# First layer's opening: normalised tiles emitted whole, and the order of projections and modulation vectors

## The chip, the cores and the metric

The kernel runs on one core of one Trainium2 chip. The metric is the device time of the whole kernel in microseconds (us); the median of three runs stands for it. TensorE (PE in the profile) does the matmuls, VectorE (DVE), ScalarE (ACT) and GpSimd (POOL) do the elementwise work, and SyncE (SP) issues most DMA transfers.

## The reference, cut to what matters

Two layers of a diffusion backbone over 512 latent tokens and 256 context tokens, 1024 features wide. Only the opening of the first layer bears on this change: a vector product that gives shift and scale for each feature, a normalisation of the tokens, and the first columns of the input projection.

```python
mod_x = silu_c @ ada_w[layer] + ada_b[layer]          # the latent tokens' vectors
mod_c = silu_cc @ ada_w[layer] + ada_b[layer]         # the context tokens' vectors
sh1, sc1, g1, sh2, sc2, g2 = [m[:, None, :] for m in jnp.split(mod_x, 6, axis=-1)]
csh1, csc1, cg1, csh2, csc2, cg2 = jnp.split(mod_c, 6, axis=-1)
hx = modulate(rmsnorm(x, norm1_g[layer]), sh1, sc1)   # h * (1 + scale) + shift
hc = modulate(rmsnorm(ctx, norm1_g[layer]), csh1, csc1)
lat, cx = project_in(hx, w_in[layer]), project_in(hc, w_in[layer])   # hx @ w_in
```

All that follows (retention, gated linear attention, output projection, the MLP, the second layer) starts from these projections.

## The kernel before, in words

Tokens lie along the free axis (768 columns: latent 0 to 511, context 512 to 767) and features along the 128 partitions, so the stream is 8 feature blocks, numbered kk. Every large matmul is done as products of a high and a low part: a weight slab is split into `hi_wi` (ScalarE, L244) and `lo_wi` (VectorE, L245), and a normalised tile into `hh_n` (ScalarE) and `hl_n` (VectorE). `project` (L443 to L447 and L459, L460) issues three matmuls for each feature block (hi x hi, hi x lo, lo x hi); for slab 0 (`RankSlab`) it issues two, L459 on `hh_n` and L460 on `hl_n`.

The first layer opens by quarters, because its modulation vectors come from 8 MB of `ada_w` that must be loaded first. A quarter q covers feature blocks 2q and 2q + 1 and has these steps:

- the vector product (`quarter`, L391): 32 matmuls of the conditioning vectors with the quarter's share of `ada_w` (eight loads of 256 KB), summed in the one bank of the pool `psa`;
- `ada_finish`: ScalarE copies the row out (`adarow`, L269), TensorE transposes it (`adat`, L274), VectorE adds the bias into `mod` (L280). It is a generator: it starts with the copy, the second tick after that emits the transposes, the third emits the additions;
- `quarter_end`: VectorE forms the scales (`mods_n`, L507);
- `quarter_norm`: queues four tile chains, latent kk = 2q and 2q + 1, then context 2q and 2q + 1. A chain (`apply`) has three steps, one a tick: x times rstd (VectorE L525, or GpSimd L518 where kk is 2 or 5), then `hh_n` on ScalarE (L527, or L520 and L521), then `hl_n` on VectorE (L529 or L523). One chain is started each tick, so four chains are wholly emitted after six ticks;
- the projections (`start_project`): slabs 0, 1 and 3, each on the latent and then on the context columns, accumulate over all four quarters in six PSUM banks (`acc0`). Below, "slab 1's block" is both groups of one slab for one quarter.

Each engine works through its own instructions in the order in which the program emits them. `project` calls `ready` on each tile first, which ticks the chains until that tile's chain is emitted, and it ends with one tick. So before this change the order of emission was, for quarters 2 and 3: vector product, row copy, then the projections of the quarter before, with the transposes and the additions emitted inside them by the ticks. For quarter 2 the four tile chains of quarter 1 were still unemitted when its vector product was issued.

SyncE issues the loads in one queue: x of the latent tokens, quarter 0, slabs 0, 1 and 3, x of the context tokens, quarters 1, 2 and 3, and then the slabs of the first token projection (`ps_vg`, slabs 5 to 8), which follows the opening. Their splits are emitted after quarter 3's tiles.

Of the kernel before, what the change touches and what calls it, by code (L numbers as in the profile page):

```python
# [138 lines left out]
def build(ctx: ExitStack, tc, a):  # L139
# [15 lines left out]
    ch = Chains()  # L155

    def bank(name):
        return ps.tile([P, 512], F32, tag="ps", name=name)
# [21 lines left out]
    ALLG = [(0, LAT), (LAT, T)]  # L180
# [84 lines left out]
    def ada_finish(l, pt, tiles, n, fold=1):  # L265

        m = 32 * fold * len(tiles)
        row = temp(f"adarow_{l}_{tiles[0]}")
        nc.scalar.copy(row[0:m, 0:n], pt[0:m, 0:n])  # L269
        yield  # L270
        yield
        tt = bank(f"adat_{l}_{tiles[0]}")
        for j in range(n // P):
            nc.tensor.transpose(tt[:, j * P : j * P + m], row[0:m, j * P : (j + 1) * P], ident[0:m, 0:m])  # L274
        yield
        src = tt.rearrange("p (j c m) -> p j c m", j=4, c=4)
        for i in range(fold * len(tiles)):
            f = tiles[i % len(tiles)]
            dst = mod[l][:, :, f : f + n // P]
            nc.vector.tensor_tensor(  # L280
                dst, src[:, 0 : n // P, i, 0:2].rearrange("p j v -> p v j"),
                dst if i >= len(tiles) else rep(adab[:, l, f : f + n // P], 2), op=ALU.add,
            )
# [99 lines left out]
    def quarter(q, middle=None, end=None):  # L383

        pt = psa.tile([P, 512], F32, tag="psa", name=f"ada0_{q}")
        for k2 in range(KK // 2):
            if k2 == 2 and middle:
                middle()
            for c in range(4):
                kk = 2 * k2 + c // 2  # L390
                nc.tensor.matmul(  # L391
                    pt[32 * c : 32 * c + 32, 0:QF], cs[:, kk, :], quarter_w[q, kk][:, c % 2],
                    start=(k2 == 0), stop=(k2 == KK // 2 - 1),
                )
        if end:
            end()
        return ch.start(ada_finish(0, pt, [2 * q, KK + 2 * q], QF, 2))
# [51 lines left out]
    def project(pt, slab, c0, acts, t0, t1, ks=None, first=0, last=None):  # L449

        ks = range(len(acts)) if ks is None else ks
        last = len(acts) - 1 if last is None else last
        out = pt[:, 0 : t1 - t0]
        for k in ks:
            acts[k].ready(ch, t0, t1)
            xh, xl = acts[k].hi[:, t0:t1], acts[k].lo[:, t0:t1]
            w = slice(c0 + k * P, c0 + k * P + P)
            if isinstance(slab, RankSlab):
                nc.tensor.matmul(out, slab.hi[:, w], xh, start=k == first, stop=False)  # L459
                nc.tensor.matmul(out, slab.hi[:, w], xl, start=False, stop=k == last)  # L460
            else:
                mm3(out, slab.hi[:, w], slab.lo[:, w], xh, xl, k == first, k == last)
        ch.tick()
# [87 lines left out]
    def squares(t0, t1, late=KK):  # L551
        for kk in range(KK):
            if kk < late:
                norm0.add_square(kk, t0, t1, kk == 0)
            else:
                norm0.late_square(kk, t0, t1)
            if kk:
                ch.tick()

    def fill(n):  # L560

        pt = bank(f"fill{n}")
        for _ in range(n):
            nc.tensor.matmul(pt[:, 0:P], ones_d, ones_d, start=True, stop=True)

    def quarter_norm(q, groups):
        for t0, t1 in groups:
            norm0.apply_all(0, 0, int(t0 > 0), t0, t1, (2 * q, 2 * q + 1))

    def quarter_end(q, chain):  # L570
        ch.finish(chain)
        norm0.scales(0, 8, n1g, 2 * q, 2 * q + 2)

    START = (0, 1, 3)
    acc0, quarter_chain = {}, {}

    def start_project(q, groups):
        for j in START:
            for t0, t1 in groups:
                if q == 0:  # L580
                    acc0[j, t0] = bank(f"ps0_{j}_{t0}")
                project(acc0[j, t0], sl0[j], 0, norm0.out, t0, t1, (2 * q, 2 * q + 1), 0, KK - 1)

    def start_norms():
        squares(0, LAT)
        end = quarter(0, lambda: norm0.stat(0, LAT))
        sl0[0].cast()
        quarter_end(0, end)
        fill(12)
        quarter_norm(0, ALLG[:1])  # L590
        for _ in range(2):
            ch.tick()
        sl0[0].low()
        for _ in range(2):
            ch.tick()
        sl0[1].split()
        sl0[3].split()
        squares(LAT, T, 5)
        start_project(0, ALLG[:1])
        norm0.stat(LAT, T)  # L600
        quarter_norm(0, ALLG[1:])
        for _ in range(6):
            ch.tick()
        end = quarter(1)
        start_project(0, ALLG[1:])
        quarter_end(1, end)
        quarter_norm(1, ALLG)
        quarter_step(2)
        quarter_finish(2)

    def quarter_step(q):
        quarter_chain[q] = quarter(q)
        start_project(q - 1, ALLG)

    def quarter_finish(q):
        quarter_end(q, quarter_chain[q])
        quarter_norm(q, ALLG)
        for _ in range(6):
            ch.tick()

    late = {}
# [46 lines left out]
    def layer(l, norm):  # L668
# [436 lines left out]
        if l == 0:  # L1105

            def head():
# [5 lines left out]

            plan = [
                Item(pre + "norm", start_norms, ahead=0),
                Item(pre + "q3", lambda: quarter_step(3), ahead=0),
                Item(pre + "q3n", lambda: quarter_finish(3), ahead=0),
                Item(pre + "q3p", lambda: start_project(3, ALLG), ahead=0),
                Item(pre + "head", head, ahead=4),
# [340 lines left out]
```

## Time and profile before

| | |
|---|---|
| median of 3 runs | 1656.87 us (1656.79 to 1657.32) |
| profiled execution: its own time | 1658.22 us |
| span in the trace | 1656.5 us |
| PE busy | 1622.8 us, 98% of the span |
| DVE, ACT, POOL busy | 943.8, 628.7, 191.9 us |
| mean granted clock of TensorE | 0.996 |
| first vector product starts | 11.92 us |
| first matmul of `ps_vg` (the opening is over) | 64.17 us |

The table's times are microseconds from the start of the span. A granted clock of 1.00 is TensorE's upper level, 2.4 GHz, and 0.50 is the lower, 1.2 GHz. A busy share says how long an engine had an instruction in work, not that it worked at its peak.

### The profile page before, as it was taken

The page shows a single profiled execution, that of the slowest core. Times are in us where ns is not written, and L with a number is a line of the kernel's source. Part 1 is how long each engine was busy: PE and PEld are TensorE (multiplying, and loading weights), DVE is VectorE, ACT ScalarE, POOL GpSimd, SP SyncE. Part 2 cuts the span into 40 slices and gives each one's busy share as a digit, 9 for nine tenths or more (in the row PEclk, how much of TensorE's full clock was granted, in tenths as well). Part 3 has the DMA queues.
Part 4 walks back from the last instruction along what each step waited for, and adds up shares of the span by engine and source line. Part 5 has one row for each costly group of instructions (what it writes and reads, how often), then busy time and mean ns, then how long its engine had stood idle before and what let it go on. Part 6 is the DMA issues. An engine that isn't in the chain of part 4 may idle for free. (4 is left out here: it accounts for less than half of the span.)

```text
span 1656.5 us, 23002 instructions
## 1 busy us (share of the span) xinstructions
PE 1622.8 (98%) x9290; PEld 1386.3 (84%) x9290; DVE 943.8 (57%) x1494; ACT 628.7 (38%) x1085; POOL 191.9 (12%) x213
## 2 busy tenths in 40 slices
PE   6999999999999999999999999999999999999997
PEld 3778788988998888888888887888889988888887
DVE  4776564554756565555556476688466743443445
ACT  4545423662542221222222247363464622222232
POOL 2000021210111000110101121002111301010010
PEclk9999999999999999999999999999999999999999
DMA  9433333123323343333333221121114323223311
GB/s 318 155 127 127 129 109 115 57 67 112 103 88 124 103 136 100 125 115 115 128 114 118 96 99 64 51 65 64 51 57 147 115 89 102 94 97 102 102 64 52
DMA packets 57483, 173.82 MB, mean 105 GB/s; under 512 B 6208, under 2 KB 17792, under 8 KB 57376
## 3 DMA queue, kind: packets, MB, share of 16 engines
q1 hardware_dynamic: 54944, 164.32, 29.9%
q0 software_dynamic: 2432, 8.03, 1.4%
q8 instruction: 73, 1.20, 0.3%
q14 instruction: 34, 0.28, 0.1%
HBM read 168.13 MB, written 4.19 MB: 104 GB/s over the span
## 5 line engine op out<-in xcount | busy, mean ns | idle before, releaser
L446 PE MATMUL pm<-yl,hi_m 128*128 128x512 f32 (+1 forms) x808 | 279.8, 346 | 1.1 <-DVE yl L523 0.7
L445 PE MATMUL pm<-yh,hi_m 128*128 128x512 f32 (+1 forms) x808 | 279.9, 346 | 0.0
L445 PE MATMUL pm<-hidh,hi_m 128*128 128x512 f32 (+1 forms) x800 | 279.1, 349 | 0.0
L447 PE MATMUL pm<-yh,lo_m 128*128 128x512 f32 (+1 forms) x808 | 278.7, 345 | 0.0
L446 PE MATMUL pm<-hidl,hi_m 128*128 128x512 f32 (+1 forms) x800 | 278.4, 348 | 0.0
L447 PE MATMUL pm<-hidh,lo_m 128*128 128x512 f32 (+1 forms) x800 | 277.3, 347 | 0.0
L1231 ACT ACTIVATE relu<-pm 128x512 f32<-128x512 f32 (+1 forms) x101 | 51.2, 507 | 494.1 <-PE pm L447 490.4
L1235 DVE TENSOR_TENSOR hidl<-relu,hidh 128x512 fp32r<-128x512 f32 (+1 forms) x101 | 61.6, 612 | 289.9 <-POOL relu L1233 289.9
L543 DVE SCALAR_TENSOR_TENSOR x<-pm,mod,x 128x512 f32<-128x512 f32 (+1 forms) x200 | 117.6, 640 | 109.0 <-PE pm L447 109.0
L1233 POOL TENSOR_TENSOR relu<-relu 128x512 f32<-128x512 f32 (+1 forms) x101 | 90.5, 897 | 756.0 <-ACT hidh L1232 755.8
L446 PEld LDWEIGHTS pm<-yl,hi_m 128*128 128x128 f32 x808 | 153.1, 189 | 20.7 <-DVE yl L529 1.2
L445 PEld LDWEIGHTS pm<-yh,hi_m 128*128 128x128 f32 x808 | 153.1, 189 | 19.9 <-issue 1.2
L445 PEld LDWEIGHTS pm<-hidh,hi_m 128*128 128x128 f32 x800 | 151.5, 189 | 21.2 <-issue 1.1
L447 PEld LDWEIGHTS pm<-yh,lo_m 128*128 128x128 f32 x808 | 153.0, 189 | 18.7
L447 PEld LDWEIGHTS pm<-hidh,lo_m 128*128 128x128 f32 x800 | 151.1, 189 | 19.6
L446 PEld LDWEIGHTS pm<-hidl,hi_m 128*128 128x128 f32 x800 | 151.5, 189 | 18.9 <-issue 0.2
L245 DVE TENSOR_TENSOR lo_m<-raw_m,hi_m 128x1024 fp32r<-128x1024 f32 x126 | 153.9, 1222 | 10.1 <-ACT hi_m L244 10.1
L244 ACT CAST hi_m<-raw_m 128x1024 fp32r<-128x1024 f32 x128 | 129.5, 1041 | 51.3 <-DMA raw_m<-in_w_mlp 28.3
L351 DVE SCALAR_TENSOR_TENSOR adaacc<-adaw,cs,adaacc 128x1024 f32<-128x1024 f32 x84 | 103.9, 1278 | 0.0
L245 DVE TENSOR_TENSOR lo_wi<-raw_wi,hi_wi 128x1024 fp32r<-128x1024 f32 x54 | 66.4, 1246 | 27.7 <-ACT hi_wi L244 27.6
L445 PE MATMUL pwo<-yh,hi_wo 128*128 128x256 f32 (+1 forms) x224 | 70.9, 316 | 0.1
L446 PE MATMUL pwo<-yl,hi_wo 128*128 128x256 f32 (+1 forms) x224 | 70.3, 314 | 0.3 <-DVE yl L1079 0.3
(307 smaller groups left out, 2937.7 us busy)
## 6 DMA issues: line engine op xcount, KB each, us to landing
raw_m<-in_w_mlp SPq DMA_DIRECT2D x128, 512.0 KB, 3.5
adaw<-in_ada_w SPq DMA_DIRECT2D x80, 512.0 KB, 3.8
raw_wi<-in_w_in SPq DMA_DIRECT2D x58, 512.0 KB, 4.2
adaw<-in_ada_w SPq DMA_DIRECT2D x32, 256.0 KB, 6.1
raw_wo<-in_w_out SPq DMA_DIRECT2D x16, 512.0 KB, 3.5
x<-in_xT POOLq DMA_DIRECT2D x8, 384.0 KB, 8.1
x<-in_xT SPq DMA_DIRECT2D x8, 256.0 KB, 5.3
raw_wob<-in_w_out SPq DMA_DIRECT2D x4, 512.0 KB, 4.4
```

The costliest lines, as they stand in the source:

```text
L244: nc.scalar.copy(self.hi, self.raw)
L245: self.engine.tensor_sub(self.lo, self.raw, f32(self.hi))
L351: nc.vector.scalar_tensor_tensor(acc[:, v], w, c, acc[:, v], op0=ALU.mult, op1=ALU.add)
L445: nc.tensor.matmul(out, wh, xh, start=first, stop=False)
L446: nc.tensor.matmul(out, wh, xl, start=False, stop=False)
L447: nc.tensor.matmul(out, wl, xh, start=False, stop=last)
L543: nc.vector.scalar_tensor_tensor(xs[kk][:, t0:t1], pt[:, 0 : t1 - t0], mod[l][:, v, gate + kk : gate + kk + 1], xs[kk][:, t0:t1], op0=ALU. ...
L1231: nc.scalar.activation(r, pt[:, 0 : t1 - t0], AF.Relu)
L1233: nc.gpsimd.tensor_mul(r, r, r)
L1235: nc.vector.tensor_sub(a_.lo[:, t0:t1], r, f32(a_.hi[:, t0:t1]))
```

## The change

`start_project` takes a list of slabs. In `quarter_step` the projections of the quarter before are cut in two: those of slabs 0 and 1 are issued ahead of the next quarter's vector product, those of slab 3 behind it. After quarter 1's tile chains are queued, eight ticks emit them whole before quarter 2's step. `quarter_finish` ticks eight times in place of six.

```diff
-    def start_project(q, groups):
-        for j in START:
+    def start_project(q, groups, slabs=START):
+        for j in slabs:
...
         quarter_norm(1, ALLG)
+        for _ in range(8):
+            ch.tick()
         quarter_step(2)
         quarter_finish(2)
 
     def quarter_step(q):
+        start_project(q - 1, ALLG, START[:2])
         quarter_chain[q] = quarter(q)
-        start_project(q - 1, ALLG)
+        start_project(q - 1, ALLG, START[2:])
 
     def quarter_finish(q):
         quarter_end(q, quarter_chain[q])
         quarter_norm(q, ALLG)
-        for _ in range(6):
+        for _ in range(8):
             ch.tick()
```

## Rows read from the trace of the kernel before

**Rows 1.** The page's busy times and shares of the span.

```profile
PE 1622.8 (98%) x9290; PEld 1386.3 (84%) x9290; DVE 943.8 (57%) x1494; ACT 628.7 (38%) x1085; POOL 191.9 (12%) x213
```

**Rows 2.** PE by stages: stage, length, busy (instructions), clock, DMA share, GB/s.

```profile
0.00:50.00 50.00, 33.70 (x198) 0.93 0.92 308
50.00:100.00 50.00, 49.73 (x265) 1.00 0.31 105
```

**Rows 3.** PE's waits after 64 us, longest: total, times, longest us.

```profile
PE ps_d L459 <- ACT hh_n L527: 1.5, 1, 1.5
```

**Rows 4.** PE's timeline of the opening: start, us, instruction [idle before, releaser].

```profile
34.43 4.43 PE L391 MATMUL ada<-adaw,cs 128*32 128x256 f32 x32
39.33 0.44 PE L274 MATMUL adat<-c_ident,adarow 128*128 128x128 f32 x2 [0.47 <-ACT adarow L269]
40.04 0.50 PE L459 MATMUL ps<-hh_n,hi_wi 128*128 128x512 f32 x1 [0.27 <-ACT hh_n L520]
41.78 0.79 PE L460 MATMUL ps<-hl_n,hi_wi 128*128 128x512 f32 x1 [1.24 <-DVE hl_n L523]
...
44.52 0.63 PE L445 MATMUL ps<-hh_n,hi_wi 128*128 128x512 f32 x1
...
50.43 1.93 PE L391 MATMUL ada<-adaw,cs 128*32 128x256 f32 x32
52.30 0.50 PE L459 MATMUL ps<-hh_n,hi_wi 128*128 128x512 f32 x1
...
53.80 0.38 PE L274 MATMUL adat<-c_ident,adarow 128*128 128x128 f32 x2
53.94 0.47 PE L445 MATMUL ps<-hh_n,hi_wi 128*128 128x512 f32 x1
...
59.97 0.39 PE L445 MATMUL ps<-hh_n,hi_wi 128*128 128x512 f32 x1
...
64.17 0.40 PE L445 MATMUL ps_vg<-hi_wi,hh_n 128*128 128x512 f32 x1
```

**Rows 5.** Weight loads' timeline, the last wait of quarter 2's product.

```profile
38.23 0.14 PEld L391 LDWEIGHTS ada<-adaw,cs 128*32 128x32 f32 x4 [0.62 <-DMA adaw<-in_ada_w]
```

**Rows 6.** VectorE's timeline of the opening.

```profile
34.28 0.23 DVE L507 SCALAR_TENSOR_TENSOR mods_n<-mod,c_n1g 128x2 f32<-128x2 f32 x2
...
43.58 0.47 DVE L529 SCALAR_TENSOR_TENSOR hl_n<-xn_n,mod,hh_n 128x256 fp32r<-128x256 f32 x1
43.98 0.22 DVE L507 SCALAR_TENSOR_TENSOR mods_n<-mod,c_n1g 128x2 f32<-128x2 f32 x2
...
48.78 0.42 DVE L523 TENSOR_TENSOR hl_n<-xn_n,hh_n 128x256 fp32r<-128x256 f32 x1 [0.44 <-ACT xn_n L521]
...
54.69 0.23 DVE L507 SCALAR_TENSOR_TENSOR mods_n<-mod,c_n1g 128x2 f32<-128x2 f32 x2
...
59.21 0.48 DVE L529 SCALAR_TENSOR_TENSOR hl_n<-xn_n,mod,hh_n 128x256 fp32r<-128x256 f32 x1 [0.18 <-ACT hh_n L527]
60.14 4.63 DVE L245 TENSOR_TENSOR lo_wi<-raw_wi,hi_wi 128x1024 fp32r<-128x1024 f32 x4 [0.45 <-ACT hi_wi L244]
```

**Rows 7.** ScalarE's timeline: quarter 1's first tile.

```profile
39.17 0.82 ACT L520 ACTIVATE hh_n<-xn_n,mod,mods_n 128x512 fp32r<-128x512 f32 x1
```

**Rows 8.** PE in half-microsecond stages where the granted clock changes; columns of rows 2.

```profile
41.00:41.50 0.50, 0.00 (x0) 0.78 1.13 367
48.00:48.50 0.50, 0.50 (x5) 0.90 0.06 25
1003.50:1004.00 0.50, 0.29 (x2) 0.84 0.27 90
1007.00:1007.50 0.50, 0.50 (x6) 0.75 0.00 0
```

**Rows 9.** PE's timeline at the second layer's opening.

```profile
995.40 0.70 PE L498 MATMUL st_n<-ssum_n,ones_d 128*128 128x256 f32 x2 [1.29 <-DVE ssum_n L481]
...
1001.29 0.38 PE L459 MATMUL ps_d<-hh_n,hi_wi 128*128 128x256 f32 x1 [1.53 <-ACT hh_n L527]
```

## The prediction

> **What bounds the kernel now.** I read the page first, then TensorE's share by stages of 50 us, then the waits, and only then the opening's timelines. TensorE is busy 98% of the span [rows 1], so time is lost or won only where it waits or runs at its lower clock. The stages say where that is: the first 50 us hold 16.3 us in which TensorE had no matmul, at a mean clock of 0.93, and the next 50 us hold 0.3 [rows 2]. Of all its waits after 64 us the longest is 1.5 us, for a tile at the second layer's opening [rows 3], and no DMA is among the releasers. Hence a shift of the point where the opening ends and `ps_vg` begins, 64.17 us [rows 4], goes through to the end of the kernel nearly one for one: no later wait for a load is there to swallow it.
>
> In the opening itself the reader sees this [rows 4]. Quarter 2's vector product takes from 34.43 to 38.86, 4.43 us for work that takes 1.93 at quarter 3, because it runs at the pace of its loads; the last of them is waited for until 38.23 [rows 5]. ScalarE's row copy of quarter 2 stands behind that product and ahead of quarter 1's tiles, so quarter 1's first `hh_n` starts only at 39.17 [rows 7]. TensorE then waits again, 1.24 us for `hl_n` [rows 4], and its clock falls: the half microsecond from 41.0 has a mean of 0.78, and the one from 48.0 a mean of 0.90 on its way up [rows 8], so it was at 0.50 from about 41.3 to 48.05. From 50.43 on TensorE has nearly no gap until 64.17: quarter 3's product, quarter 2's six projections with quarter 3's transposes inside them, quarter 3's projections.
>
> So two things are to be weighed: the stretch of 10.1 us from 34.43 to 44.52, in which TensorE does a product and slab 0's block only, and the cover that the later quarters have now.
>
> **Step 1: quarter 1's tiles come earlier.** With the tiles emitted before the vector product, the row copy no longer stands ahead of them. They need the scales, which end at 34.28 + 0.23 = 34.51 [rows 6]. Before, the four tiles took from 39.17 [rows 7] to 43.58 + 0.47 = 44.05 [rows 6], 4.88 us, with ScalarE and VectorE in turn. From 34.55 that gives 39.43. Slab 1's block starts 0.28 us behind the last tile (59.21 + 0.48 = 59.69 to 59.97 [rows 6, 4]), so at 39.7 where it was 44.52: 4.8 us won. GpSimd's products need no scales and stay off this path.
>
> **Step 2: two blocks, the product, one block.** At the upper clock the blocks of slabs 1 and 3 take 64.17 - 59.97 = 4.20 us together [rows 4], 2.10 each. A product with its weights present takes 52.30 - 50.43 = 1.87 [rows 4], and quarter 2's are present from about 38.3 [rows 5]. So 39.7 + 2.10 + 1.87 + 2.10 puts quarter 2's transposes at 45.8. The wait for the loads is covered.
>
> **Step 3: what is late next.** `ada_finish` emits its transposes on its second tick and its additions on the third. Behind the product there are now two projections, hence two ticks, so the transposes come behind all of the quarter's projections and nothing is left on TensorE to cover what follows them: additions, scales, four tiles. All of quarter 2's projections stand behind that in TensorE's queue, and so do quarter 3's product and everything later. The price comes from before, where the same chain ran under cover. From transposes to scales: 54.69 - 53.80 = 0.89 [rows 6, 4]. From quarter 2's scales to its last tile: 48.78 + 0.42 - 43.98 = 5.22 [rows 6]. With the 0.28 of step 1 that is 6.4 us until slab 1's block, in which TensorE has only its transposes and slab 0's block to do (53.80 - 52.30 = 1.50 [rows 4]): about 4.7 us of new idle time. Block, product and block (6.07) put quarter 3's transposes at 45.8 + 6.4 + 6.1 = 58.3. Quarter 3's chain from transposes to slab 1's block took 59.97 - 53.80 = 6.17 [rows 4], which gives 64.4, and two blocks of 2.10 end the opening at 68.6. At the upper clock throughout, the change costs 68.6 - 64.17 = 4.4 us: it wins 4.8 once and some of the first clock loss, and then pays two gaps of 4.5 to 4.7 that were under cover.
>
> **Step 4: the clock.** Two falls in this trace give the price. In the opening the blocks of slabs 1 and 3 took 50.43 - 44.52 = 5.91 in place of 4.20 [rows 4], a loss of 1.7. At the second layer the clock fell at about 1003.8 and rose at about 1007.25 [rows 8], 3.4 us of dense matmuls at half speed, again 1.7. It fell there after a wait of 1.53 us at 1001.29 with lone matmuls behind it, while a single wait of 1.29 at 995.40 did not bring it down [rows 9]. The new order has three stretches of 5 to 6 us (after the projections of quarters 0, 1 and 2, each up to the last tile of the next quarter) in which TensorE is idle for 3.8, 4.7 and 4.5 us: each idles longer than either stretch before which the clock fell. I count three falls. Bounds for each: nothing, if it does not fall, and 3.4, if dense work meets all of a low stretch as long as the opening's 6.8 us. I take 2.0, near the two rows, a little above as the blocks behind each gap are longer than those at the second layer. Three times 2.0 is 6.0; what before lost to its own fall is already in the 64.17.
>
> The Trainium skill, "TensorE: Matmul & The Clock Gate", section "HAM oscillation — how this bites in real kernels", speaks against this change: bursts with waits between them make every burst start at the lower clock, and the cost is paid at each. By that rule the sum is the whole 4.4 + 6.0; by the 995.40 row alone, where a wait passed without a fall, it is 4.4.
>
> **Edits at nothing.** The two extra ticks in `quarter_finish` find the four chains done. No DMA is added or moved on SyncE's queue or GpSimd's. The splits of slabs 5 to 8 follow quarter 3's last tile (60.14 for 4.63 us [rows 6]) and move with it; `ps_vg` keeps its distance to them, since two blocks still lie between. If that cover failed, each split would show as up to 1.2 us of wait (4.63 / 4).
>
> **The sum.** 4.4 + 6.0 = 10.4 us. On the profiled execution, 1658.22 (span 1656.5), that is 1668.6; its own time lies 1.35 above the median, so on the median of 1656.87 the forecast is 1667.3.
>
> **The rivals.** (a) The gaps come, but TensorE's clock stays up, or falls once: 4.4 to 6.4 us, 1661.3 to 1663.3. For it: lone matmuls break each gap, the first stretch is the only one like the one that fell before, and a wait of 1.29 us passed [rows 9]. Against it: the idle sums above. (b) The falls are long ones, each near 3.4: 14.6 us, 1671.5. For it: the opening's own low stretch was that long [rows 8]. Against: half of such a stretch falls into waiting. (c) Faster: the transposes' chain is covered after all, so that only step 1 works. Then the opening ends at 45.8 + slab 0's block, block, product, block (7.6) + slab 0's block and two blocks (5.7) = 59.1, about 5 us earlier, 1651.8. It turns on the two gaps: below 2.4 us each the change would win. Against it: after its transposes TensorE has no instruction that does not need a tile of that quarter, and the first `hh_n` alone needs additions, scales, one product and one ScalarE pass. (d) No change to speak of: the gaps come out at half their price with no fall, or a later wait swallows the shift; 1657 to 1660. Against it: [rows 2, 3].
>
> **How the numbers follow.** The forecast 0.61, (a) 0.18, (b) 0.12, (c) 0.04, (d) 0.05. A measurement here tells about 0.2%, 3.3 us, from no change; so slower has 0.61 + 0.18 + 0.12 = 0.91, the same 0.05, faster 0.04. The forecast's own range is 1664.5 to 1670. The range given runs from below (a), with the gaps some tenths cheaper, to (b): 1660.5 to 1671.5.
>
> **What would show it.** Step 1: quarter 1's first `hh_n` near 34.6, slab 1's block near 39.7 to 40. Step 2: quarter 2's product with no wait for DMA, in 1.9 us (up to double at the lower clock). Step 3: two stretches, each starting at L274, with some 2.2 us of no matmul until `hh_n` and the rest of the idle time behind `hl_n`. Step 4: three stretches of granted clock 0.50 before 75 us. `ps_vg` starts near 74.6. The prediction is wrong if transposes stand ahead of a block, if `ps_vg` starts by 66, or if the shift at `ps_vg` is not that at the end.

## The result, and the profile after

The changed kernel takes 1667.14 us (median of 4 runs, 1666.03 to 1668.68) against 1656.83 for the kernel before: 10.3 us slower, a ratio of 1.0063 with a 95% interval of 1.0046 to 1.0081. The forecast was 1667.3. The profiled execution of the changed kernel took 1666.81, that of before 1658.22, so the two traced executions differ by 8.6 us and not by 10.3; the section on the prediction comes back to this.

TensorE's timeline of the opening, changed kernel (start, us, instruction, idle before and its releaser):

```profile
35.35 0.49 PE L459 MATMUL ps<-hh_n,hi_wi 128*128 128x512 f32 x1 [0.92 <-ACT hh_n L520]
36.93 0.50 PE L460 MATMUL ps<-hl_n,hi_wi 128*128 128x512 f32 x1 [1.08 <-DVE hl_n L523]
...
39.35 0.39 PE L460 MATMUL ps<-hl_n,hi_wi 128*128 128x256 f32 x1 [1.13 <-DVE hl_n L523]
...
40.82 0.63 PE L445 MATMUL ps<-hh_n,hi_wi 128*128 128x512 f32 x1
...
44.07 1.93 PE L391 MATMUL ada<-adaw,cs 128*32 128x256 f32 x32
...
48.17 0.38 PE L274 MATMUL adat<-c_ident,adarow 128*128 128x128 f32 x2
50.80 0.50 PE L459 MATMUL ps<-hh_n,hi_wi 128*128 128x512 f32 x1 [2.26 <-ACT hh_n L527]
...
54.72 0.63 PE L445 MATMUL ps<-hh_n,hi_wi 128*128 128x512 f32 x1
...
57.87 1.93 PE L391 MATMUL ada<-adaw,cs 128*32 128x256 f32 x32
...
61.94 0.38 PE L274 MATMUL adat<-c_ident,adarow 128*128 128x128 f32 x2
64.58 0.49 PE L459 MATMUL ps<-hh_n,hi_wi 128*128 128x512 f32 x1 [2.26 <-ACT hh_n L527]
...
68.26 0.63 PE L445 MATMUL ps<-hh_n,hi_wi 128*128 128x512 f32 x1
...
71.38 0.40 PE L445 MATMUL ps<-hh_n,hi_wi 128*128 128x512 f32 x1
...
73.48 0.40 PE L445 MATMUL ps_vg<-hi_wi,hh_n 128*128 128x512 f32 x1
```

These rows answer to [rows 4]. Quarter 2's vector product at 44.07 takes 1.93 us with no wait for a load, where it took 4.43. Quarter 1's first tile meets TensorE at 35.35, where it was 40.04. Then come two stretches that were not there before: behind the transposes at 48.17 and at 61.94 TensorE has no matmul for 2.26 us, waits again inside slab 0's block, and reaches slab 1's block 6.55 and 6.32 us after the transposes. `ps_vg` starts at 73.48, 9.3 us later.

TensorE by stages of the changed kernel (stage, length, busy, granted clock, DMA share, GB/s):

```profile
40.00:50.00 10.00, 8.12 (x60) 0.84 0.67 253
50.00:60.00 10.00, 8.10 (x53) 0.83 0.10 28
60.00:70.00 10.00, 6.95 (x27) 0.85 0.00 1
```

The mean clock is 0.83 to 0.85 in each of three stages: it fell three times in this execution, each time for about 3.4 us, where the opening of the kernel before has one fall of 6.8 us [rows 8]. Slab 1's block, 2.10 us at the upper clock, takes 44.07 - 40.82 = 3.25, 57.87 - 54.72 = 3.15 and 71.38 - 68.26 = 3.12.

### The profile page after: what moved, and what is told of

The parts are those of the page before. It is cut to its first block, busy times and chain, and to the rows that moved or that the text cites. A ratio compares the mean times of both kernels' runs of the same rounds, so it can differ in the third digit from the quotient of the medians.

```text
span 1665.0 us, 23000 instructions
## 1 busy us (share of the span) xinstructions
PE 1624.1 (98%) x9290; PEld 1387.4 (83%) x9290; DVE 945.3 (57%) x1494; ACT 629.1 (38%) x1085; POOL 192.0 (12%) x213
```

## The experiments

Each kernel was timed together with the kernel before, whose medians were 1655.8 to 1656.7; the ratios are to these. Each edit is shown against the changed kernel, that of e6 against e1. All keep the eight ticks of `quarter_finish`, so no run tests these by themselves.

**e1: the early tiles without the new order.**

```diff
     def quarter_step(q):
-        start_project(q - 1, ALLG, START[:2])
         quarter_chain[q] = quarter(q)
-        start_project(q - 1, ALLG, START[2:])
+        start_project(q - 1, ALLG)
```

> Only the eight ticks that emit quarter 1's tiles whole; the vector product stands ahead of all six projections again. Theory (the new order uncovers the chain behind the transposes, the early tiles win time): slab 1's block of quarter 1 near 40.8 us in place of 44.52, no gap behind the transposes of quarters 2 and 3, ps_vg near 59 to 61, kernel at 1652 to 1654. Rival A (the early tiles themselves cost: TensorE idles before slab 1's block and its clock falls there): 1657 to 1660, not below the kernel before.

Measured: 1652.7 us (1652.2 to 1653.45), ratio to before 0.9976 (0.9967 to 0.9986). TensorE's timeline of e1, and its stage with the clock:

```profile
34.09 3.46 PE L391 MATMUL ada<-adaw,cs 128*32 128x256 f32 x32
...
40.40 0.38 PE L274 MATMUL adat<-c_ident,adarow 128*128 128x128 f32 x2
40.54 0.48 PE L445 MATMUL ps<-hh_n,hi_wi 128*128 128x512 f32 x1
...
44.92 1.93 PE L391 MATMUL ada<-adaw,cs 128*32 128x256 f32 x32
...
48.32 0.38 PE L274 MATMUL adat<-c_ident,adarow 128*128 128x128 f32 x2
...
58.68 0.40 PE L445 MATMUL ps_vg<-hi_wi,hh_n 128*128 128x512 f32 x1
```

```profile
40.00:50.00 10.00, 9.82 (x76) 1.00 0.77 279
```

The product is paced by its loads again (3.46 us), but it now runs while quarter 1's tiles are made, so slab 1's block starts at 40.54 in place of 44.52 [rows 4]. The transposes stand ahead of that block, two blocks (four projections) of cover follow, there is no gap behind them, and the clock stays at 1.00 in the opening. The early tiles win 4.0 us; rival A, that they cost, is out.

**e2: the new order without the eight ticks.**

```diff
         quarter_norm(1, ALLG)
-        for _ in range(8):
-            ch.tick()
         quarter_step(2)
```

> Only the new order of projections, without the eight ticks behind quarter 1's chains. Theory: the projections emit the tiles by their own ticks ahead of the product, so nothing moves: the same two gaps of 4.5 to 5 us behind the transposes, ps_vg near 73.5, 1666 to 1668. Rival A (the ticks carry the cost): near the kernel before, 1657 to 1659.

Measured: 1667.47 us (1666.55 to 1668.48), ratio 1.0066 (1.0051 to 1.0081). TensorE's timeline of e2:

```profile
47.91 0.38 PE L274 MATMUL adat<-c_ident,adarow 128*128 128x128 f32 x2
50.55 0.50 PE L459 MATMUL ps<-hh_n,hi_wi 128*128 128x512 f32 x1 [2.26 <-ACT hh_n L527]
...
73.25 0.40 PE L445 MATMUL ps_vg<-hi_wi,hh_n 128*128 128x512 f32 x1
```

The same gap of 2.26 us and nearly the same end of the opening (73.25 against 73.48). The order carries the whole loss; with projections in front of the product, the eight ticks change nothing that is seen here, because `project` emits the tiles that it needs.

**e3: one slab in front of the product, two behind.**

```diff
-        start_project(q - 1, ALLG, START[:2])
+        start_project(q - 1, ALLG, START[:1])
         quarter_chain[q] = quarter(q)
-        start_project(q - 1, ALLG, START[2:])
+        start_project(q - 1, ALLG, START[1:])
```

> One slab's projections ahead of the product, two behind it. Theory: two ticks after the product are now those of slab 1's block, so the transposes come ahead of slab 3's block and its 2.1 us cover a part of each chain: idle time of each gap down by about 2.1, ps_vg 4 to 5 us earlier than with the change, near 69, 1661 to 1663. Rival B (the loss is the lower clock alone, and any gap brings it): within 1 us of the change, 1666 to 1668.

Measured: 1661.82 us (1661.08 to 1663.53), ratio 1.0033 (1.002 to 1.0046). TensorE's timeline of e3:

```profile
47.07 0.38 PE L274 MATMUL adat<-c_ident,adarow 128*128 128x128 f32 x2
...
49.71 0.50 PE L459 MATMUL ps<-hh_n,hi_wi 128*128 128x512 f32 x1 [0.17 <-ACT hh_n L527]
...
68.01 0.40 PE L445 MATMUL ps_vg<-hi_wi,hh_n 128*128 128x512 f32 x1
```

Slab 3's block lies between the transposes and the first tile's matmul, and the wait for that tile is 0.17 in place of 2.26. The clock falls in the first stretch alone, there for 6.8 us. Rival B is out: not every gap brings a fall, and two falls fewer are worth some 2 us (an estimate from e4 below, 3.1 us for three), less than the 5.3 us won here.

**e4: matmuls to hold the clock in the gaps.**

```diff
         quarter_norm(1, ALLG)
+        fill(12)
         for _ in range(8):
             ch.tick()
...
         quarter_end(q, quarter_chain[q])
+        fill(14)
         quarter_norm(q, ALLG)
```

> The change with matmuls on constants, whose output nothing reads, in the three gaps (12 behind quarter 0's projections, 14 behind the scales of quarters 2 and 3), so that TensorE has something to do while it waits. Theory by the trace of the change: the granted clock stays at 1.00, slab 1's three blocks take 2.1 us in place of 3.15 to 3.25, 3 us in all, ps_vg near 70.3, 1663 to 1665; the gaps themselves stay. Rival B (the loss is the lower clock alone): back to 1657 to 1659.

Measured: 1664.01 us (1663.35 to 1664.3), ratio 1.0045 (1.0029 to 1.0062). TensorE's timeline of e4, and its stages with the clock:

```profile
40.39 0.40 PE L445 MATMUL ps<-hh_n,hi_wi 128*128 128x512 f32 x1
...
42.58 1.93 PE L391 MATMUL ada<-adaw,cs 128*32 128x256 f32 x32
...
46.65 0.38 PE L274 MATMUL adat<-c_ident,adarow 128*128 128x128 f32 x2
47.65 3.36 PE L564 MATMUL fill<-ones_d 128*128 128x128 f32 x28 [0.61 <-DVE mod L280]
...
53.06 0.40 PE L445 MATMUL ps<-hh_n,hi_wi 128*128 128x512 f32 x1
...
69.70 0.40 PE L445 MATMUL ps_vg<-hi_wi,hh_n 128*128 128x512 f32 x1
```

```profile
40.00:50.00 10.00, 9.23 (x80) 1.00 0.66 250
50.00:60.00 10.00, 9.35 (x76) 1.00 0.10 26
60.00:70.00 10.00, 9.54 (x62) 1.00 0.21 65
```

The clock stays at 1.00 and slab 1's first block takes 42.58 - 40.39 = 2.19. The gaps stay: from the transposes to slab 1's block it is 53.06 - 46.65 = 6.41 us, and 6.17 the second time. So the falls cost 1667.14 - 1664.01 = 3.1 us, and some 7 us of the loss is there without any fall.

**e5: the changed order with the transposes right behind the product.**

```diff
         quarter_chain[q] = quarter(q)
+        for _ in range(2):
+            ch.tick()
         start_project(q - 1, ALLG, START[2:])
```

> The change with two ticks right behind the vector product, so that the transposes of quarters 2 and 3 stand ahead of slab 3's block and everything else keeps its place. Theory (the place of the transposes is what uncovers the chain): slab 3's block covers 2.1 us of each chain, less the wait for the row copy of about 0.5; each gap shrinks by about 1.6 to 2.1, the clock need not fall behind the shorter ones, ps_vg near 67.5 to 70, 1660.5 to 1663.5. Rival C (the projections in front of the product cost by themselves, wherever the transposes stand): 1666 to 1668 as with the change.

Measured: 1662.72 us (1662.04 to 1663.19), ratio 1.0042 (1.0028 to 1.0056). TensorE's timeline of e5:

```profile
44.47 1.93 PE L391 MATMUL ada<-adaw,cs 128*32 128x256 f32 x32
46.90 0.44 PE L274 MATMUL adat<-c_ident,adarow 128*128 128x128 f32 x2 [0.49 <-ACT adarow L269]
...
49.60 0.49 PE L459 MATMUL ps<-hh_n,hi_wi 128*128 128x512 f32 x1 [0.17 <-ACT hh_n L527]
...
53.36 0.39 PE L445 MATMUL ps<-hh_n,hi_wi 128*128 128x512 f32 x1
...
55.55 1.93 PE L391 MATMUL ada<-adaw,cs 128*32 128x256 f32 x32
...
64.20 0.40 PE L445 MATMUL ps<-hh_n,hi_wi 128*128 128x512 f32 x1
...
68.39 0.40 PE L445 MATMUL ps_vg<-hi_wi,hh_n 128*128 128x512 f32 x1
```

Two ticks, and no projection moved: 4.4 us come back. The transposes now wait 0.49 for the row copy, and slab 3's block covers 2.1 us of the chain. From a quarter's product to the next slab 1's block it is 53.36 - 44.47 = 8.89 and 64.20 - 55.55 = 8.65 us, where the changed kernel took 54.72 - 44.07 = 10.65 and 68.26 - 57.87 = 10.39: 3.5 us in all. The clock falls in the first stretch alone, and the blocks behind the other two take 2.19 and 2.09 in place of 3.15 and 3.12. Rival C is out for that part; the rest of the loss stays, since one block of cover is not the two that e1 has there.

**e6: e1 with feature block 5 off GpSimd.**

```diff
-                c = ch.queue(self.apply(kk, l, shift, v, t0, t1, kk % 3 == 2))
+                c = ch.queue(self.apply(kk, l, shift, v, t0, t1, kk % 3 == 2 and (self.name, kk) != ("n1_0", 5)))
```

> The kernel with the early tiles alone, and feature block 5 of the first norm normalised on VectorE and ScalarE in place of GpSimd. Claim under test: VectorE's 128x256 product at 37.2 us took 1.5 us in place of 0.48 because GpSimd's product ran beside it. If so it takes 0.48 here, quarter 1's last tile comes about 1 us earlier, TensorE's two waits of 0.3 and 0.5 us in slab 0's block go, and the kernel is 0.5 to 1 us faster than with the early tiles alone, 1651.5 to 1652.5. If another cause made it long, it stays at 1.5 and nothing moves.

Measured: 1651.66 us (1650.6 to 1652.86), ratio 0.9972 (0.9962 to 0.9981), the fastest version here. Its interval overlaps that of e1, and the kernel before, too, was 0.8 us faster when timed with e6 than with e1 (1655.83 against 1656.67), so the medians do not set the two apart; the traces do. VectorE's timeline of e6:

```profile
37.85 0.48 DVE L525 SCALAR_TENSOR_TENSOR xn_n<-x,mods_n,ssum_n 128x256 f32<-128x256 f32 x1
...
38.90 0.48 DVE L529 SCALAR_TENSOR_TENSOR hl_n<-xn_n,mod,hh_n 128x256 fp32r<-128x256 f32 x1 [0.17 <-ACT hh_n L527]
```

The product takes 0.48 in place of 1.5, and TensorE has no wait left in the opening from quarter 2's product to `ps_vg`.

**e7: the same edit on the changed kernel.** The diff is that of e6.

> The change with feature block 5 of the first norm on VectorE and ScalarE in place of GpSimd. It tests the size of step 1 in the changed order itself: without GpSimd's product beside it, quarter 1's tiles should take the 4.9 us that they took before (4.76 with the early tiles alone) in place of 6.15, slab 1's first block should start 1.2 to 1.4 us earlier after the scales, and the kernel should come out 1 to 2 us below the change, 1665 to 1666.5; the two gaps and the three falls of the clock stay. If quarter 1's tiles stay at 6.1 us, something other than GpSimd's product made them late.

Measured: 1664.3 us (1662.59 to 1664.71), ratio 1.0047 (1.003 to 1.0064): 2.8 us below the change, more than expected. VectorE's and TensorE's timelines of e7:

```profile
33.41 0.23 DVE L507 SCALAR_TENSOR_TENSOR mods_n<-mod,c_n1g 128x2 f32<-128x2 f32 x2
...
36.64 0.48 DVE L525 SCALAR_TENSOR_TENSOR xn_n<-x,mods_n,ssum_n 128x256 f32<-128x256 f32 x1
...
37.70 0.48 DVE L529 SCALAR_TENSOR_TENSOR hl_n<-xn_n,mod,hh_n 128x256 fp32r<-128x256 f32 x1 [0.17 <-ACT hh_n L527]
```

```profile
38.46 0.40 PE L445 MATMUL ps<-hh_n,hi_wi 128*128 128x512 f32 x1
```

The scales of quarter 1 started at 33.41 in that run, so its tiles were done after 4.8 us and slab 1's block began after 5.05, where the changed kernel needed 40.82 - 34.23 = 6.59. In this profile the clock also did not fall in the first stretch, which accounts for about 1 us more. So "the three falls stay" was wrong for this execution. It is the fastest of the four by 1.5 us, with a mean clock of 0.996 where the others have 0.995; whether the first fall is gone in those too is not shown.

## Why the prediction was right, and which terms were mis-sized

**Bound and propagation: right.** `ps_vg` moved by 9.3 us and the span by 8.5 (1656.5 to 1665.0). Nearly all of the shift reached the end; the 0.8 between them went mostly by 152 us, where the first `ps_gq` matmuls stand 8.6 us later (151.82 against 143.24).

**Step 1, early tiles: right in kind, 1.1 us too short.** "GpSimd's products need no scales and stay off this path" is the sentence that failed. VectorE's and GpSimd's timelines of the changed kernel:

```profile
34.23 0.23 DVE L507 SCALAR_TENSOR_TENSOR mods_n<-mod,c_n1g 128x2 f32<-128x2 f32 x2
...
37.46 1.50 DVE L525 SCALAR_TENSOR_TENSOR xn_n<-x,mods_n,ssum_n 128x256 f32<-128x256 f32 x1
...
39.54 0.84 DVE L529 SCALAR_TENSOR_TENSOR hl_n<-xn_n,mod,hh_n 128x256 fp32r<-128x256 f32 x1 [0.24 <-ACT hh_n L527]
```

```profile
36.95 1.72 POOL L518 TENSOR_TENSOR xn_n<-x,ssum_n 128x512 f32<-128x512 f32 x1 [6.34 <-DVE hl_n L523]
39.37 0.73 POOL L518 TENSOR_TENSOR xn_n<-x,ssum_n 128x256 f32<-128x256 f32 x1 [0.70 <-DVE hl_n L523]
```

GpSimd's product of quarter 2 is released as soon as quarter 1's first `hl_n` frees its buffer, and runs just when VectorE has quarter 1's context tiles to do. VectorE's product took 1.50 and its last tile 0.84, where both take 0.48 in e6. From the start of the scales the tiles took 6.15 us (34.23 to 39.54 + 0.84), where the forecast had 39.43 - 34.28 = 5.15 and e7 took 4.77. Slab 1's block started at 40.82 in place of 39.7, 1.1 us late. GpSimd's product costs more than that, 1.4 us (6.15 against 4.77), because the 4.88 that the forecast took over from the kernel before held some of it already. There the same kind of pair ran side by side, in VectorE's and GpSimd's timelines of the kernel before:

```profile
42.71 0.95 DVE L523 TENSOR_TENSOR hl_n<-xn_n,hh_n 128x256 fp32r<-128x256 f32 x1
```

```profile
42.47 0.91 POOL L518 TENSOR_TENSOR xn_n<-x,ssum_n 128x256 f32<-128x256 f32 x1 [1.29 <-DVE hl_n L529]
```

VectorE's took 0.95 there and takes 0.42 in e7. The Trainium skill, "SBUF — State Buffer", section "Who interferes with whom", states it: a VectorE instruction with two SBUF inputs and a GpSimd instruction that reads SBUF contend for a read port that they share, and the second to issue blocks until the first is done. The trace fits this: VectorE's product, issued 0.5 us behind GpSimd's, ends 0.3 behind its end at 38.67, and the pair above ends 0.3 apart as well.

**Step 2, the wait for the loads: right.** 1.93 us with no wait, as in the forecast. That wait was worth little once the tiles came early: in e1 the product is paced by its loads (3.46 us), and the tiles that TensorE would wait for anyway are made meanwhile.

**Step 3, the place of the transposes: right, and the cause of the loss.** From transposes to slab 1's block 6.4 and 6.17 us were forecast; 6.55 and 6.32 were measured, slab 0's last matmuls being at the lower clock; e4, where the clock stays up, has 6.41 and 6.17. The idle time inside was smaller than the forecast's 4.7: of the 6.18 us from 48.54 to 54.72 TensorE was busy for 2.83 in place of some 1.5, since slab 0's matmuls run one by one and partly at the lower clock; what counts is the length of the chain. e5 moves the transposes alone and wins 4.4 us, e3 moves one block and wins 5.3, both with two falls of the clock fewer; e2 shows that quarter 1's ticks have no part in it, and e1 puts the product in front again and wins 14.4.

**Step 4, the clock: three falls, as forecast, at half the price.** 6.0 us were allowed, 3.1 measured (e4). This is the term that was mis-sized most: 2.0 a fall, where slab 1's blocks in the trace lost 3.25 - 2.10 = 1.15, 1.05 and 1.02. Both rows used as the price gave 1.7, the one at the second layer from 3.4 us of dense matmuls at half speed. The low stretches of the changed kernel are 3.4 us long too, but the clock falls (at about 39.7, 53.4 and 67.0) while TensorE still waits for slab 0's tiles, so only 2.1 to 2.3 us of each meets slab 1's block. The rule of the Trainium skill that the prediction cites is told there of one long DMA wait between two bursts; no gap here is of that kind, each is broken by single matmuls. Behind all three gaps of the changed kernel the next block did start at the lower clock. Behind the two shortened ones of e3 and e5 it did not: the clock was 1.00 from 50 to 70 us.

Where a fall comes and how long it lasts is not fixed by the program alone. e5 gives TensorE the same instructions as the changed kernel up to the end of quarter 2's product, yet its clock was low from about 37.3 for 6.8 us, against 39.7 and 3.4 us. And of the changed kernel's four timed executions the two with mean clocks of 0.995 took 1666.03 and 1666.81 us, those with 0.994 and 0.993 took 1667.48 and 1668.68.

**The sum came out by cancelling, and its closeness is luck.** On the two traces the forecast for `ps_vg` was 10.4 us and the shift 9.3. Step 1 was short by 1.1, the two chains by 0.15 each, the two products with slab 3's blocks by 0.1 each, and the clock's term was 2.8 too large: 10.4 + 1.1 + 0.3 + 0.2 - 2.8 = 9.2. Of that shift 8.5 reached the end, so the profiled execution took 1666.81 where the sum gave 1668.6, 1.8 too much. On the medians this error is hidden. The profiled execution of before (1658.22) was slower than every timed one (1655.06 to 1658.11) and 1.4 above the median, that of the changed kernel 0.3 below its own, so the medians lie 10.3 apart and not 8.6. The excess of the trace of before seems to lie in its opening, from which every bound was taken: against e1 both `ps_vg` and the end of the span differ by 5.5 us, the medians only by 4.0. No second trace of before was taken, so this part is open.

**The rivals.** (a), the gaps with no fall, would have given 1661.3; with the clock held (e4) the kernel took 1664.0. In e4's trace the steps cost 69.70 - 64.17 = 5.5 us at `ps_vg` in place of 4.4, most of the difference in step 1; the rest of its error is the distance of the traces from the medians. (b), long falls each near 3.4 us of loss, is not in the profiled execution; the mean clocks of 0.994 and 0.993 above suggest that some falls were longer in others. (c), faster, needed gaps below 2.4 us, and TensorE idled 2.26 us before the first tile alone and 3.4 in all in the first of the two. (d), 1657 to 1660, is out by the measured time.

## What to carry to other kernels

Before an order is changed to fill one wait, look for what the moved work was covering: here two blocks moved ahead of a product filled a wait for loads that was worth little once the tiles came early, and took the cover from a chain of transposes, additions, scales and tiles that runs twice. Where generators emit work by ticks, count the ticks between a chain's start and its next use, because moving a call moves every instruction that the ticks emit. When a price for the lower clock is taken from a trace, count only the matmuls that would not have waited anyway.

## What was not expected of the hardware

A GpSimd product of 128x512 made a VectorE product of 128x256 with two inputs take 1.50 us in place of 0.48, and cost the kernel's opening 1.4 us in the traces (e7). With the same three gaps, 12 short fp32 matmuls on constants in the first and 14 in each of the others held the granted clock at 1.00 from 30 to 70 us, for 3.1 us of gain (e4). With the same instructions before it, the clock fell at 37.3 us for 6.8 us in one execution (e5) and at 39.7 for 3.4 us in another (the changed kernel).
